# The first stage of a two-block float32 kernel: all 1024 columns of v at once, tile by tile of x

## The chip, the cores and the metric

The kernel runs on one core of a Trainium2 chip. The metric is device microseconds for one execution. Five engines work side by side, each through its own instructions in order: TensorE (PE) for matrix products, VectorE (DVE) and ScalarE (ACT) for elementwise work, GpSimd (POOL), and SyncE (SP), which here issues transfers. They wait for one another through semaphores.

## What is computed

One sequence of 256 tokens with 1024 channels goes through two blocks in float32. The first block has two layers of attention and a feed-forward with a short convolution, the second one a gated delta rule, a retention branch and a feed-forward. The change concerns the start of the first layer:

```python
h = rmsnorm(x, attn_norm[l])
q, k, v = jnp.split(h @ w_qkv_a[l], 3, axis=-1)
q = partial_rope(heads(q, N_HEADS), cos, sin)
k = partial_rope(heads(k, N_HEADS), cos, sin)
o = moba_attention(to_bhsd(q), to_bhsd(k), to_bhsd(heads(v, N_HEADS)))
```

`rmsnorm` multiplies x by a gain per channel and a factor per token, 1/sqrt(mean(x^2) + eps). The angles of the rotation come from `positions`. With 256 tokens the attention is a causal softmax over one block of keys.

## The kernel before

**Products.** x lies transposed on chip, `xT`, as 8 tiles of 128 channels by 256 tokens. Every float32 operand of a large product is split in two parts, hi and lo, and a product is three passes on PE: hi by hi, hi by lo, lo by hi. The weights, 212 MB in all, stream through four buffers `raw` (one transfer fills one, 128x1024 or, at the start, 128x512). ACT makes hi (`emit_hi`, line 188), DVE makes lo by 512 columns (`emit_lo`, line 197), into four buffers each; `ahead` keeps this stream some pieces in front of PE. The parts of x times gain lie in OH and OL.

**Order.** Each engine works through its instructions in the order in which the program's Python issues them. The loop at the end takes a weight piece, issues its products, then lets every running side task (a generator) go one step (`others`), then works ahead on weights. A task's `yield from pause(n)` lets n pieces pass. The tables N_SY and N_STAT say how many pieces the norm's task `stat` lets pass ahead of its sums and ahead of its row products.

**First stage.** x comes in four transfers of two tiles; its gains, `g_attn0`, come with the first parameters in a transfer on ACT's queue. `feed_x` multiplies two tiles by the gain on DVE into TG, splits them, and squares x. The first 512 columns of v take both halves of the tokens over the eight tiles (`X_pair`, two banks of PSUM, `ps_w`), the other 512 follow as two chunks of 256 (`X_chunk`). Meanwhile `stat` sums the squares on PE, makes `tok` on DVE and the factor RTOK on GpSimd, and multiplies RTOK out into rows on PE, which ACT copies to RB. v is evacuated by ACT with the factor RTOK. `angles` makes the angle tables CT and ST in side steps, on DVE with two sines on ACT, then the masks.

**Next stage.** Eight chunks `wqk0` give q and k of two heads each (`W_chunk`). `rope_rows` multiplies the angle tables by RB into CR and SR, `rope` (lines 583 to 586) rotates a chunk on DVE with them, and `attend` does scores, softmax and the product with v, its banks taken from `ps_s` or `ps_d` in turn. The scores of chunks 0 and 1 follow half of chunk 2 on PE.

Of the kernel before, what the change touches and what calls it, by code (L numbers as in the profile page):

```python
# [30 lines left out]
# steps that side work lets pass before it needs what others make for it  # L31
N_RN = (0, 1, 1, 5)
N_SY = (0, 6, 4, 4, 3)
N_STAT = (0, 3, 5, 2, 5)
# [3 lines left out]
N_M1 = (1, 1, 2, 3)  # L38
# [4 lines left out]
PRM = [("g_attn0", 8), ("g_attn1", 8), ("g_kv", 8), ("g_ffn0", 8), ("g_ffn1", 8), ("g_fin", 8),  # L43
# [22 lines left out]
def body(ctx: ExitStack, tc: tile.TileContext, a):  # L66
# [27 lines left out]
    xT = T1([128, 8, T], name="xT")  # L94
# [14 lines left out]
    # the gains first, then x; what is needed later comes behind the first weights  # L109
    nc.scalar.dma_start(prm[:, :PRM_A], a["prm"][:, :PRM_A])  # L110

    def load_x(b):
        nc.sync.dma_start(xT[:, 2 * b:2 * b + 2], a["x"][:, 2 * b:2 * b + 2])
    load_x(0)
    ident = C_("ident")
    ones = T1([128, 1], name="ones")
    V.memset(ones, 1.0)
    warm = T1([128, 1], name="warm")
# [89 lines left out]
    def ahead(i):  # L208
        """what may be loaded and split once the products of piece i are issued"""
# [50 lines left out]
    # tiles that are held over steps: no more of them than the ring has  # L260
# [17 lines left out]
    def wbank(more=0):  # L278
        """two banks in turn; two more while the norm's factors are on their way"""
        if len(deferred) >= 4:  # L280
            drain(cur["stat"])
            late(1)
        wn[0] += 1
        if len(deferred) + more >= 2 and wn[0] % 4 in (3, 0):
            return PT("d")
        return PT("w")

    wn = [0]
# [58 lines left out]
    def N_chunk(src, xs, n, post):  # L347
        """n < 128 columns in a piece"""
# [14 lines left out]
    def D_chunk(grp, src, c, n, ops, post=None, pre=None, done=None):  # L363
        def m(ck, s, hi, lo):
            if c == 0:
                if s == 0:
                    grp.banks = [None] * 4
                    side["dbusy"] = True
                grp.banks[s] = PT("d")
# [20 lines left out]
    def D_tail(grp, src, n, ops, post, pre=None):  # L390
        """the last two chunks, a bank after the other"""
# [18 lines left out]
    def W_pair(src, xs, posts):  # L410
        """two chunks of outputs at once, over the tiles of x"""
# [23 lines left out]
    def X_pair(src, xs, posts):  # L435
        """512 columns, a bank for each half of the tokens"""
# [20 lines left out]

    def slots(t):
        return OH[:, t % 16], OL[:, t % 16]

# [5 lines left out]
    def split(src, hi, lo):  # L466
        """the second part a step after the first"""
# [25 lines left out]
    def sum_ch(out, parts):  # L493
        """sums over the channels, a token per partition; 32 tokens at a time, as the weights' load is what they take"""
# [19 lines left out]
    def renorm():  # L514
        """the splits of x * g * r, for the chunks after the first"""
# [73 lines left out]
    # over the keys of two blocks, for the queries of the second: all of the first, or with the window  # L589
# [4 lines left out]
    # key > query: column > partition  # L594
# [16 lines left out]
    def attend(q, k, v, slot, window=False, sink=None, delay=0, done=False):  # L611
        """q, k: [128, T], a head on each half of the partitions; v(t, half) -> [128, 64]"""
# [38 lines left out]
        for h in range(2):  # L651
# [3 lines left out]
            # blocks: (q0, k0), (q1, k0), (q1, k1)  # L655
# [11 lines left out]
    # ================= the first block =================  # L667
# [7 lines left out]
    def feed_x(b, g, xs, norm, norm2=None, g2=None, first=False):  # L675
        """after xT's pair b is complete: x * g and its splits, the squares"""
        s = slice(2 * b, 2 * b + 2)
        for k in (2 * b, 2 * b + 1):
            cp("V" if first else "V", TG[:, k], xT[:, k], g[:, k:k + 1])
        S.activation(xs[0][:, s], TG[:, s], AF.Copy)  # L680
        if not first:
            sq = square(xT[:, s], norm.room(b))
# [4 lines left out]
        if first:  # L687
            yield
        else:
            yield from pause(3)  # L690
        V.tensor_tensor(xs[1][:, s], TG[:, s], xs[0][:, s].bitcast(F32), op=OP.subtract)
        if first:
            yield
            sq = square(xT[:, s], norm.room(b))
# [13 lines left out]
    # attention of layer 0  # L708
    def v0_pair(t):
        return lambda bank: cp("S", VA[:, t, 0:512], bank, RTOK[:, t:t + 1])  # L710

    def v0_post(c):
        def f(bank):
            for t in range(2):
                S.activation(VA[:, t, c * 256:c * 256 + 256], bank[:, t * T:t * T + T], AF.Copy,
                             scale=RTOK[:, t:t + 1])
        return f
# [15 lines left out]
    X_pair(a["wv0p"], xsR, [v0_pair(t) for t in range(2)])  # L733
    for c in range(2, 4):
        X_chunk(a["wv0"][c - 2], xsR, v0_post(c))
    for j in range(8):
        W_chunk(a["wqk0"][j], xsR, qk0_post(j))
# [30 lines left out]
    def tables():  # L768
        """of the second block"""
# [9 lines left out]
    # feed-forward with a short convolution  # L779
# [63 lines left out]
    # attention of layer 1  # L843
# [45 lines left out]
    # ================= between the blocks =================  # L889
# [7 lines left out]
    def stat2():  # L897
# [4 lines left out]
        # r1 = 1 / sqrt(mean x^2 + eps), and r1 r2 with r2 the factor of x g r1  # L902
# [23 lines left out]
    # ================= the second block =================  # L926
# [10 lines left out]
    def decay_task(bank):  # L937
        # beta and g, a token per partition
# [63 lines left out]
    def conv4(src, u, y, base):  # L1002
        """src, u, y: [128, 2, T]; tiles base[i] of conv_a"""
# [37 lines left out]
    # the small blocks on the diagonal, and the transposes of the inverses  # L1041
# [4 lines left out]
    def delta_task(h, bank):  # L1046
# [180 lines left out]
    # gates of the two branches; they take the decays' place  # L1227
# [10 lines left out]
    # retention  # L1238
# [141 lines left out]
    # residual with a norm behind it: x += y * g * rsqrt(mean(y^2) + eps)  # L1380
# [26 lines left out]
    def to_tok(src, s, banks):  # L1407
        """two tiles of src, a token per partition"""
# [20 lines left out]
    def mix_fin():  # L1429
# [18 lines left out]
        # the first two tiles one by one  # L1448
# [15 lines left out]
    def res_task():  # L1464
# [9 lines left out]
        # the factor r of the feed-forward comes in as r^2: eps / r^4 stands in the norm behind  # L1474
# [17 lines left out]
    # the last feed-forward; its input's factor r comes in at the end, as r^2  # L1492
# [16 lines left out]
    # the products of the last step come with a token per partition, those of its last chunks a half after the other  # L1509
# [61 lines left out]
    # ================= emission =================  # L1571
    # the first pieces of the weights one by one, with the tiles of x between them
    chunks[0].g = 1
    order()
    load_w()
    load_w()
    load_x(1)
    load_w()
    load_w()
    load_x(2)  # L1580
    load_x(3)
    nc.scalar.dma_start(cst[:, :CST_A], a["cst"][:, :CST_A])
    nc.scalar.dma_start(SR.bitcast(I32), a["pos"])
    # the first tiles of x and of the weights by turns
    def more(n):
        for _ in range(n):
            ahead(-1)
    for b in range(4):
        feed(b, P_("g_attn0"), xsR, n0, first=True)
        more(1)  # L1590
        step(fed[b])
        more(N_M1[b])
        if b >= 1:
            drain(fed[b - 1])
    start_stat(n0)
    while ahead(-1):
        pass
    cur["ang"] = start(angles())
# [18 lines left out]
def pack(inp):  # L1617
# [5 lines left out]
    def wc(w, cols):  # L1623
        """[1024, 256 columns] -> [128, 2048]"""
# [5 lines left out]
    def dset(w):  # L1630
        """[K, 1024] -> [K/256, 128, (bank, k tile, 256)]"""
# [4 lines left out]
    def pair(w, cols):  # L1636
        """[1024, 512 columns] -> two of [128, (4 k tiles, 512)]"""
# [6 lines left out]
    def dsett(name, w):  # L1644
        """the last 512 rows as [2, 128, (bank, 4 k tiles, 256)]"""
# [6 lines left out]
    out["x"] = np.ascontiguousarray(A("x")[0].T.reshape(8, 128, T).transpose(1, 0, 2))  # L1652
    out["pos"] = np.ascontiguousarray(np.broadcast_to(A("positions")[0].astype(np.int32)[None], (128, T)))
    w = A("w_qkv_a")[0]
    wsetp("wv0", w, [2048 + 256 * c + r(256) for c in range(4)])
# [44 lines left out]
    def row(v):  # L1700
# [10 lines left out]
        "g_attn0": vec(A("attn_norm")[0]), "g_attn1": vec(A("attn_norm")[1]), "g_kv": vec(A("kv_norm")),  # L1711
# [58 lines left out]
```

## Time and profile before

| | us |
|---|---|
| three runs | 1341.1, 1344.09, 1344.65 |
| median | 1344.09 |
| profiled execution, first to last instruction (its span) | 1341.2 |
| PE busy in it | 1317.4 |
| DVE busy | 984.4 |
| ACT busy | 731.6 |

The page gives the profiled execution by its span alone. In the profile a row of a timeline is a group of equal instructions: its start, how long from its start to the end of its last one, engine, source line, operation, output<-inputs, shapes and count, and in brackets idle time before it with what ended it. Rows of engines overlap, and so do equal instructions that follow each other. PEclk is the clock that PE was granted, as a share of 2.4 GHz.

### The profile page before, as it was taken

The numbers are of one execution on the slowest core, as the hardware profiler recorded it, in microseconds if no ns is written. First come the engines' busy times: TensorE is split into PE (matmuls) and PEld (weight loads), VectorE is DVE, ScalarE is ACT, GpSimd is POOL, SyncE is SP. The second block draws the span as 40 slices with busy tenths as digits, with TensorE's granted clock in tenths as the row PEclk, the third lists the DMA queues.
The fourth block names the chain that finished last, engine by engine and source line by source line (L and its number), as shares of the span: only waits on it lengthen the run. The fifth ranks groups of instructions, "written<-read, shape, count | busy, mean of one in ns | idle before, by whom it ended". The sixth has DMA issues, their size and how long they took to land.

```text
span 1341.2 us, 29103 instructions
## 1 busy us (share of the span) xinstructions
PE 1317.4 (98%) x11824; PEld 1250.3 (93%) x11824; DVE 984.4 (73%) x2225; ACT 731.6 (55%) x1202; POOL 27.2 (2%) x38
## 2 busy tenths in 40 slices
PE   7999999999999999999999999999999999999998
PEld 6999999998889999999888888999999999999996
DVE  6997887778878877788778888666557556855554
ACT  6665765555765655566545544444343445655553
POOL 0000000000000000000000000000000000000000
PEclk9999999998999999999999999999999999999999
DMA  7435565554334655544333333445455564465652
GB/s 240 156 127 183 175 205 188 186 181 142 107 117 156 215 189 189 185 133 158 115 107 114 110 126 104 134 157 191 150 179 168 173 196 153 160 219 184 189 183 89
DMA packets 60470, 215.79 MB, mean 161 GB/s; under 512 B 6832, under 2 KB 7600, under 8 KB 60336
## 3 DMA queue, kind: packets, MB, share of 16 engines
q1 hardware_dynamic: 59328, 212.31, 49.1%
q8 instruction: 93, 1.52, 0.5%
q10 hardware_dynamic: 1008, 1.63, 0.4%
q14 instruction: 41, 0.34, 0.1%
HBM read 212.86 MB, written 1.05 MB: 159 GB/s over the span
## 4 chain that ended last, share of the span: by engine, by line
PE 92%; DVE 4%; ACT 2%; issue 1%; DMA 1%; POOL 0%; SPq 0%; POOLq 0%; DVEq 0%; ACTq 0%
PE ps_w L134 54%; PE ps_d L134 33%; PE ps_s L134 4%; PE ps_s L145 1%; ACT h L634 1%; DVE lo L197 1%; PE ps_d L145 1%; DMA xT<-in_x 0%; DMA raw<-in_wv0p 0%; DVE y L794 0%; ACT hi L188 0%; DVE XL L464 0%; DVE h L626 0%; DVE y L1369 0%; DVE DD L1082 0%
## 5 line engine op out<-in xcount | busy, mean ns | idle before, releaser
L197 DVE TENSOR_TENSOR lo<-raw,hi 128x512 fp32r<-128x512 f32 x801 | 519.7, 684 | 93.5 <-ACT hi L188 92.7
L188 ACT ACTIVATE hi<-raw 128x1024 fp32r<-128x1024 f32 (+1 forms) x403 | 418.1, 1046 | 168.9 <-PE ps_w L134 85.7
L134 PE MATMUL ps_w<-XH,hi 128*128 128x256 f32 x976 | 168.3, 295 | 2.5 <-ACT XH L1454 1.4
L134 PE MATMUL ps_w<-XL,hi 128*128 128x256 f32 x976 | 156.3, 283 | 0.0
L134 PE MATMUL ps_w<-XH,lo 128*128 128x256 f32 x976 | 156.1, 282 | 0.0
L134 PE MATMUL ps_w<-OH,hi 128*128 128x256 f32 x896 | 144.8, 284 | 0.0
L134 PE MATMUL ps_w<-OH,lo 128*128 128x256 f32 x896 | 142.9, 282 | 0.3 <-DVE lo L197 0.3
L134 PE MATMUL ps_w<-OL,hi 128*128 128x256 f32 x896 | 142.5, 281 | 0.0
L134 PEld LDWEIGHTS ps_w<-XH,hi 128*128 128x128 f32 x976 | 134.4, 191 | 7.8 <-ACT XH L1454 1.7
L134 PEld LDWEIGHTS ps_w<-XL,hi 128*128 128x128 f32 x976 | 133.8, 190 | 0.0
L134 PEld LDWEIGHTS ps_w<-XH,lo 128*128 128x128 f32 x976 | 133.6, 190 | 0.0
L134 PE MATMUL ps_d<-OH,hi 128*128 128x256 f32 x776 | 126.0, 283 | 0.0
L134 PEld LDWEIGHTS ps_w<-OH,hi 128*128 128x128 f32 x896 | 121.5, 188 | 3.6 <-issue 3.5
L134 PE MATMUL ps_d<-OL,hi 128*128 128x256 f32 x776 | 124.4, 281 | 0.0
L134 PE MATMUL ps_d<-OH,lo 128*128 128x256 f32 x776 | 124.3, 281 | 0.0
L134 PEld LDWEIGHTS ps_w<-OH,lo 128*128 128x128 f32 x896 | 122.1, 189 | 0.5 <-DVE lo L197 0.5
L134 PEld LDWEIGHTS ps_w<-OL,hi 128*128 128x128 f32 x896 | 121.7, 188 | 0.0
L134 PEld LDWEIGHTS ps_d<-OH,hi 128*128 128x128 f32 x776 | 104.9, 188 | 1.9 <-issue 1.7
L134 PEld LDWEIGHTS ps_d<-OL,hi 128*128 128x128 f32 x776 | 105.1, 187 | 0.3 <-DVE OL L470 0.2
L134 PEld LDWEIGHTS ps_d<-OH,lo 128*128 128x128 f32 x776 | 105.1, 188 | 0.2
L790 ACT ACTIVATE y<-u,prm 128x256 f32<-128x256 f32 x88 | 48.0, 595 | 62.4 <-DVE u L764 62.4
L764 DVE TENSOR_TENSOR u<-ps_w,RB 128x512 f32<-128x512 f32 x44 | 30.1, 689 | 63.0 <-PE ps_w L134 56.8
(378 smaller groups left out, 1644.7 us busy)
## 6 DMA issues: line engine op xcount, KB each, us to landing
raw<-in_wu SPq DMA_DIRECT2D x108, 512.0 KB, 4.2
raw<-in_wd SPq DMA_DIRECT2D x68, 512.0 KB, 3.9
raw<-in_wgb SPq DMA_DIRECT2D x24, 512.0 KB, 3.7
raw<-in_wqk SPq DMA_DIRECT2D x16, 512.0 KB, 4.0
raw<-in_wza SPq DMA_DIRECT2D x16, 512.0 KB, 3.8
raw<-in_wqkb SPq DMA_DIRECT2D x16, 512.0 KB, 4.1
raw<-in_wbra SPq DMA_DIRECT2D x16, 512.0 KB, 4.2
raw<-in_wbrb SPq DMA_DIRECT2D x16, 512.0 KB, 4.7
```

The costliest lines, as they stand in the source:

```text
L134: PE.matmul(out, lhsT, rhs, start=start, stop=stop, skip_group_check=True)
L145: PE.transpose(out, in_, ident)
L188: S.activation(hi[:, :w], raws[n][:, :w], AF.Copy)
L197: V.tensor_tensor(lo[:, c], raws[n][:, c], hi[:, c].bitcast(F32), op=OP.subtract)
L634: S.activation(e[h][:, c], e[h][:, c], AF.Exp, bias=nm[:, i:i + 1], accum_out=sums[:, i:i + 1])
L764: V.tensor_tensor(u, v2(bank), bc(RB, 2), op=OP.mult)
L790: S.activation(y[:, i], u[:, i], AF.Identity, bias=P_(cb, t), scale=P_(cw, 3 * t + 2))
```

## The change

- v's 1024 columns are worked on together, x tile by x tile (`X_quad`): four banks, two of `ps_w` and two of `ps_d`, for two halves of the tokens and two halves of the columns. They are all evacuated at the end of the stage. The first chunk of q and k takes a bank of `ps_d`.
- The gains of the first norm stand in front of x in one array. The first transfer brings them with tile 0; then come tile 1, tiles 2 and 3, and tiles 4 to 7, with weights between. The remaining parameters, constants and positions follow on SP's queue, where they were on ACT's.
- OH and OL are made from x (`split_gain`): ACT multiplies by the gain while it converts, DVE makes the low part in one instruction. Tiles 0 to 3 are split ahead of the loop, tiles 4 to 7 and all squares are steps of a side task, `feed_first`.
- Two float32 products of a vector of ones, 128 by 512, which nothing reads, stand first on PE.
- N_SY and N_STAT of the first norm are 1 and 2, before 6 and 3. Banks while a norm's factors are awaited are chosen by another rule (`wbank`); outside the first layer this changes no instruction's place.

The core of the diff (comments that were taken out are not shown):

```diff
-N_SY = (0, 6, 4, 4, 3)
-N_STAT = (0, 3, 5, 2, 5)
+N_SY = (0, 1, 4, 4, 3)
+N_STAT = (0, 2, 5, 2, 5)
-N_M1 = (1, 1, 2, 3)
+WARM = 2
+X_FIRST = 4
...
-    xT = T1([128, 8, T], name="xT")
+    xg = T1([128, 8 + 8 * T], name="xT")
+    xT = xg[:, 8:].rearrange("p (k t) -> p k t", k=8)
...
-    nc.scalar.dma_start(prm[:, :PRM_A], a["prm"][:, :PRM_A])
-    def load_x(b):
-        nc.sync.dma_start(xT[:, 2 * b:2 * b + 2], a["x"][:, 2 * b:2 * b + 2])
-    load_x(0)
+    def load_x(k, n):
+        c = slice(8 + k * T if k else 0, 8 + (k + n) * T)
+        nc.sync.dma_start(xg[:, c], a["x"][:, c])
+    load_x(0, 1)
...
+    idle = PT("s")
+    for _ in range(WARM):
+        PE.matmul(idle, ones.to_broadcast([128, 128]), ones.to_broadcast([128, 512]), start=True, stop=True, skip_group_check=True)
...
-        if len(deferred) >= 4:
+        if len(deferred) + more >= 6:
             drain(cur["stat"])
-            late(1)
-        wn[0] += 1
-        if len(deferred) + more >= 2 and wn[0] % 4 in (3, 0):
-            return PT("d")
-        return PT("w")
+            late()
+        return PT("w" if len(deferred) + more < 2 else "d")
...
+    def X_quad(src, xs, posts):
+        xh, xl = xs
+        banks = {}
+        def mk(k0):
+            def m(ck, s, hi, lo):
+                k, g = k0 + s // 2, s % 2
+                todo = []
+                for t in range(2):
+                    if k == 0:
+                        banks[t, g] = PT("d" if g else "w")
+                    tt = slice(t * 128, t * 128 + 128)
+                    todo.append((banks[t, g], xh[:, k, tt], xl[:, k, tt], hi, lo, k == 0, k == 7))
+                products(todo, True)
+            return m
+        def done(ck):
+            drain(cur["stat"])
+            for g in range(2):
+                for t in range(2):
+                    wpost(posts[t, g])(banks[t, g])
+        first = add(Chunk(src[:, :1024], 1024, 2, mk(0)))
+        first.g = 1
+        add(Chunk(src[:, 1024:], 7168, 14, mk(1), None, {13: done}))
...
+    def feed_first():
+        def sq(b):
+            n0.feed(b, square(xT[:, 2 * b:2 * b + 2], n0.room(b)))
+        for k in range(X_FIRST, 8):
+            split_gain(k, xg[:, k:k + 1], xsR[0][:, k], xsR[1][:, k])
+            yield
+            if k % 2:
+                sq(k // 2 - 2)
+            yield
+        for b in range(2, 4):
+            sq(b)
+            yield
+        start_stat(n0)
...
-    X_pair(a["wv0p"], xsR, [v0_pair(t) for t in range(2)])
-    for c in range(2, 4):
-        X_chunk(a["wv0"][c - 2], xsR, v0_post(c))
+    X_quad(a["wv0"], xsR, {(t, g): v0_post(t, g) for t in range(2) for g in range(2)})
     for j in range(8):
-        W_chunk(a["wqk0"][j], xsR, qk0_post(j))
+        W_chunk(a["wqk0"][j], xsR, qk0_post(j), None, "d" if j == 0 else None)
...
+    for k, n in ((1, 1), (2, 2), (4, 4)):
+        load_w()
+        if k == 1:
+            load_w()
+        load_x(k, n)
+    nc.sync.dma_start(prm[:, :PRM_A], a["prm"][:, :PRM_A])
+    nc.sync.dma_start(cst[:, :CST_A], a["cst"][:, :CST_A])
+    nc.sync.dma_start(SR.bitcast(I32), a["pos"])
+    for k in range(X_FIRST):
+        split_gain(k, xg[:, k:k + 1], xsR[0][:, k], xsR[1][:, k])
+        for _ in range(4 if k == 0 else 2):
+            ahead(-1)
     while ahead(-1):
         pass
+    cur["stat"] = start(feed_first())
```

How the order moves is seen at three places. First SP's queue at the start of the program (in_x is x, in_wv0p and in_wv the weights of v, prm parameters, cst constants, SR the positions). Before:

```order
L113 DMA xT<-in_x 128x512
L182 DMA raw<-in_wv0p 128x512 x2
L113 DMA xT<-in_x 128x512
L182 DMA raw<-in_wv0p 128x512 x2
L113 DMA xT<-in_x 128x512 x2
L182 DMA raw<-in_wv0p 128x1024 x2
```

and now:

```order
L114 DMA xT<-in_x 128x264
L187 DMA raw<-in_wv 128x512 x2
L114 DMA xT<-in_x 128x256
L187 DMA raw<-in_wv 128x1024
L114 DMA xT<-in_x 128x512
L187 DMA raw<-in_wv 128x1024
L114 DMA xT<-in_x 128x1024
L1607 DMA prm<-in_prm 128x64
L1608 DMA cst<-in_cst 128x384
L1609 DMA SR<-in_pos 128x256
L187 DMA raw<-in_wv 128x1024 x4
```

The constants and positions now stand in front of the fifth weight transfer, which is the first 128x1024 row behind them.

Second, DVE around `tok`, from which RTOK is made (lines 559 to 569 before, 588 to 598 now, are the angles; lo<-raw,hi is the stream of weights). Before, from the first 128x1024 weights on:

```order
L197 TENSOR_TENSOR lo<-raw,hi 128x512 x4
L559 CAST CT<-SR 128x256
L560 TENSOR_SCALAR ST<-CT,prm 128x256
L197 TENSOR_TENSOR lo<-raw,hi 128x512 x3
L537 TENSOR_SCALAR tok_274<-ps_s 128x2
L197 TENSOR_TENSOR lo<-raw,hi 128x512 x2
L562 TENSOR_SCALAR CR<-ST 128x256
L563 TENSOR_SCALAR CR<-CR 128x256
```

and now, from the last fold of the squares on:

```order
L516 TENSOR_TENSOR nacc<-nacc 128x256
L591 TENSOR_SCALAR CR<-ST 128x256
L592 TENSOR_SCALAR CR<-CR 128x256
L202 TENSOR_TENSOR lo<-raw,hi 128x512 x4
L595 SCALAR_TENSOR_TENSOR ST<-CR,ST 128x256 x3
L596 TENSOR_SCALAR ST<-ST 128x256
L597 SCALAR_TENSOR_TENSOR CT<-ST 128x256
L598 TENSOR_SCALAR CT<-CT 128x256
L566 TENSOR_SCALAR tok_339<-ps_s 128x2
L202 TENSOR_TENSOR lo<-raw,hi 128x512 x6
```

`tok` stood behind two instructions of the angles and now stands behind all of them.

Third, ACT from the copy of RB on (line 188 before and 193 now convert weights; REG<-ps evacuates v; CT and ST are the two sines). Before:

```order
L542 COPY RB<-ps_s 128x256
L138 ACTIVATE REG<-ps_w,RTOK 128x512 x2
L188 ACTIVATE hi<-raw 128x1024
L715 ACTIVATE REG<-ps_d,RTOK 128x256 x2
L188 ACTIVATE hi<-raw 128x1024 x2
L571 ACT_TABLE_LOAD
L571 ACTIVATE CT<-CT 128x256
L572 ACTIVATE ST<-ST 128x256
L715 ACTIVATE REG<-ps_w,RTOK 128x256 x2
L188 ACTIVATE hi<-raw 128x1024 x5
```

and now:

```order
L571 COPY RB<-ps_s 128x256
L193 ACTIVATE hi<-raw 128x1024
L600 ACT_TABLE_LOAD
L600 ACTIVATE CT<-CT 128x256
L601 ACTIVATE ST<-ST 128x256
L143 ACTIVATE REG<-ps_w,RTOK 128x512 x2
L143 ACTIVATE REG<-ps_d,RTOK 128x512 x2
L193 ACTIVATE hi<-raw 128x1024 x5
```

The evacuations stood apart, conversions between them, the first two ahead of the sines; now all four stand in a row behind the sines.

## Rows read from the trace of the kernel before

**Rows 1.** The page: busy shares of the engines, and the conversion of weights on ACT.

```profile
PE 1317.4 (98%) x11824; PEld 1250.3 (93%) x11824; DVE 984.4 (73%) x2225; ACT 731.6 (55%) x1202; POOL 27.2 (2%) x38
...
L188 ACT ACTIVATE hi<-raw 128x1024 fp32r<-128x1024 f32 (+1 forms) x403 | 418.1, 1046 | 168.9 <-PE ps_w L134 85.7
```

**Rows 2.** Timeline of the start: start us, us to the end, engine, line, instruction.

```profile
4.33 0.62 DVE L142 TENSOR_SCALAR REG<-xT,prm 128x256 f32<-128x256 f32 x2 [3.38 <-DMA prm<-in_prm]
...
5.53 0.63 ACT L188 ACTIVATE hi<-raw 128x512 fp32r<-128x512 f32 x1
...
6.21 1.22 PE L134 MATMUL ps_w<-hi,OH 128*128 128x512 f32 x2 [6.21 <-ACT hi L188]
...
9.79 1.05 PE L134 MATMUL ps_w<-hi,OL 128*128 128x512 f32 x2
...
10.65 1.05 PE L134 MATMUL ps_w<-lo,OH 128*128 128x512 f32 x2
...
15.98 2.50 DVE L197 TENSOR_TENSOR lo<-raw,hi 128x512 fp32r<-128x512 f32 x4 [0.24 <-ACT hi L188]
...
16.00 0.73 PE L134 MATMUL ps_w<-hi,OH 128*128 128x512 f32 x2 [1.11 <-ACT hi L188]
...
17.50 0.63 PE L134 MATMUL ps_w<-hi,OH 128*128 128x512 f32 x2
...
17.96 0.63 PE L134 MATMUL ps_w<-hi,OL 128*128 128x512 f32 x2
```

**Rows 3.** What the DMA engines moved, GB/s in 40 slices of 1 us from 0.

```profile
GB/s 0 33 177 300 313 358 405 352 373 430 373 332 307 209 256 338 205 72 201 315 205 315 229 254 369 238 274 307 225 234 4 0 0 139 324 291 287 217 250 82
```

**Rows 4.** Timeline from the norm's sums to the first use of q and k.

```profile
20.39 0.22 PE L134 MATMUL ps_s<-ones,nacc 128*32 128x1 f32 x2
...
21.30 0.72 PE L134 MATMUL ps_w<-hi,OH 128*128 128x512 f32 x2
...
21.65 1.08 POOL L538 TENSOR_TENSOR RTOK<-tok,mhalf 128x2 f32<-128x2 f32 x1 [21.21 <-DVE tok L537]
...
26.01 0.37 ACT L542 COPY RB<-ps_s 128x256 f32<-128x256 f32 x1 [1.53 <-PE ps_s L145]
...
26.28 1.27 ACT L138 ACTIVATE REG<-ps_w,RTOK 128x512 f32<-128x512 f32 x2
...
29.14 1.34 DVE L566 SCALAR_TENSOR_TENSOR ST<-CR,ST 128x256 f32<-128x256 f32 x3
...
31.30 0.29 DVE L569 TENSOR_SCALAR CT<-CT 128x256 f32<-128x256 f32 x1
...
32.28 1.28 ACT L571 ACT_TABLE_LOAD   x1
...
34.22 0.63 PE L134 MATMUL ps_w<-OH,hi 128*128 128x256 f32 x4
34.42 0.84 ACT L715 ACTIVATE REG<-ps_w,RTOK 128x256 f32<-128x256 f32 x2
...
36.85 0.35 DVE L574 TENSOR_SCALAR ST<-ST,prm 128x256 f32<-128x256 f32 x1
...
40.34 0.74 DVE L583 STREAM_SHUFFLE u<-ps_w 128x512 f32<-128x512 f32 x1
...
45.78 0.01 DVE L583 LOAD_MASK_SELECT u<-ps_w  x1 [0.40 <-PE ps_w L134]
...
48.50 1.03 PE L134 MATMUL ps_d<-qk 64*128 64x128 f32 x9
```

**Rows 5.** Windows of 1 us: busy us of each engine (instructions), PEclk, DMA share, GB/s.

```profile
323.00:324.00 1.00, 0.00 (x0) 0.00 (x0) 1.00 (x3) 0.00 (x0) 0.99 (x1) 1.00 0.79 180
324.00:325.00 1.00, 0.00 (x0) 0.00 (x0) 0.67 (x2) 0.00 (x0) 1.00 (x1) 1.00 0.86 332
...
326.00:327.00 1.00, 1.00 (x9) 1.00 (x8) 0.76 (x2) 1.00 (x3) 0.00 (x0) 0.73 0.83 156
...
333.00:334.00 1.00, 1.00 (x10) 1.00 (x9) 1.00 (x2) 0.68 (x1) 0.00 (x0) 0.86 0.00 0
```

More of the change, by code (lines that the diff above doesn't have):

```diff
@@ L41 @@
 QB_HEADS = [(p, 4 + p) for p in range(4)] + [(8 + p, 12 + p) for p in range(4)]
-PRM = [("g_attn0", 8), ("g_attn1", 8), ("g_kv", 8), ("g_ffn0", 8), ("g_ffn1", 8), ("g_fin", 8),
+PRM = [("g_attn1", 8), ("g_kv", 8), ("g_ffn0", 8), ("g_ffn1", 8), ("g_fin", 8),
        ("g_mixpre", 8), ("g_mixpost", 8), ("g_mlppre", 8),
@@ L278, in wbank @@
     def wbank(more=0):
-        if len(deferred) >= 4:
+        if len(deferred) + more >= 6:
             drain(cur["stat"])
-            late(1)
-        wn[0] += 1
-        if len(deferred) + more >= 2 and wn[0] % 4 in (3, 0):
-            return PT("d")
-        return PT("w")
-    wn = [0]
+            late()
+        return PT("w" if len(deferred) + more < 2 else "d")
     def waiting():
@@ L366, in m @@
                 if s == 0:
+                    if deferred:
+                        drain(cur["stat"])
+                        late()
                     grp.banks = [None] * 4
@@ L456, in X_pair @@
         add(Chunk(src[1], 2048, 4, mk(1), None, {3: done}))
+    def X_quad(src, xs, posts):
[13 more added lines that the diff above has]
+        def done(ck):
+            drain(cur["stat"])
+            for g in range(2):
[4 more added lines that the diff above has]
+        add(Chunk(src[:, 1024:], 7168, 14, mk(1), None, {13: done}))
     def slots(t):
@@ L673, in body, with feed_x @@
     fed = {}
-    def feed_x(b, g, xs, norm, norm2=None, g2=None, first=False):
+    def feed_x(b, g, xs, norm, norm2=None, g2=None):
         s = slice(2 * b, 2 * b + 2)
         for k in (2 * b, 2 * b + 1):
-            cp("V" if first else "V", TG[:, k], xT[:, k], g[:, k:k + 1])
+            cp("V", TG[:, k], xT[:, k], g[:, k:k + 1])
         S.activation(xs[0][:, s], TG[:, s], AF.Copy)
-        if not first:
-            sq = square(xT[:, s], norm.room(b))
+        sq = square(xT[:, s], norm.room(b))
         if norm2:
@@ L686, in feed_x @@
                 S.activation(sq2[:, i * T:i * T + T], xT[:, 2 * b + i], AF.Square, scale=g2[:, 2 * b + i:2 * b + i + 1])
[L687 to L690, printed above, removed]
+        yield from pause(3)
         V.tensor_tensor(xs[1][:, s], TG[:, s], xs[0][:, s].bitcast(F32), op=OP.subtract)
-        if first:
-            yield
-            sq = square(xT[:, s], norm.room(b))
         norm.feed(b, sq)
@@ L706, in body, with v0_post @@
     n0 = Norm()
[L709 to L717, printed above, removed]
+    def feed_first():
[11 more added lines that the diff above has]
+        start_stat(n0)
+    def v0_post(t, g):
+        return lambda bank: cp("S", VA[:, t, 512 * g:512 * g + 512], bank, RTOK[:, t:t + 1])
     att = {}
@@ L1569, in body @@
         m_down(c)
-    chunks[0].g = 1
     order()
[L1575 to L1586, printed above, removed]
-            ahead(-1)
[L1588 to L1595, printed above, removed]
+    for k, n in ((1, 1), (2, 2), (4, 4)):
[9 more added lines that the diff above has]
+        for _ in range(4 if k == 0 else 2):
+            ahead(-1)
     while ahead(-1):
         pass
+    cur["stat"] = start(feed_first())
     cur["ang"] = start(angles())
@@ L1651, in pack @@
     out = {}
-    out["x"] = np.ascontiguousarray(A("x")[0].T.reshape(8, 128, T).transpose(1, 0, 2))
+    x = A("x")[0].T.reshape(8, 128, T).transpose(1, 0, 2).reshape(128, -1)
+    out["x"] = np.ascontiguousarray(np.concatenate([A("attn_norm")[0].reshape(8, 128).T, x], axis=1))
     out["pos"] = np.ascontiguousarray(np.broadcast_to(A("positions")[0].astype(np.int32)[None], (128, T)))
     w = A("w_qkv_a")[0]
-    wsetp("wv0", w, [2048 + 256 * c + r(256) for c in range(4)])
+    out["wv0"] = np.ascontiguousarray(w[:, 2048:].reshape(8, 128, 1024).transpose(1, 0, 2).reshape(128, -1))
     out["wqk0"] = wset(w, [np.concatenate([128 * j + r(128), 1024 + 128 * j + r(128)]) for j in range(8)])
@@ L1710, in pack @@
     vals = {
-        "g_attn0": vec(A("attn_norm")[0]), "g_attn1": vec(A("attn_norm")[1]), "g_kv": vec(A("kv_norm")),
+        "g_attn1": vec(A("attn_norm")[1]), "g_kv": vec(A("kv_norm")),
         "g_ffn0": vec(A("ffn_norm")[0]), "g_ffn1": vec(A("ffn_norm")[1]), "g_fin": vec(A("final_norm")),
```

## Prediction

> **What bounds the kernel now.** I read the page's busy shares first: TensorE (PE) is busy 98% of the span [rows 1]. So the change pays only if it ends a PE wait or a slow stretch of PE, and if what PE gains is not waited away behind it. Then the timeline of the start. PE's first product begins at 6.21 us, released by the first converted weight piece (0.63 on ACT, from 5.53). Two products of 128x512 start every 0.86 us there (9.79, 10.65), which is the 1.2 GHz level, though the profile's clock column reads 1.00 in that stretch; from 17.50 to 17.96 two take 0.46, the 2.4 GHz level. PE waits 1.11 us before 16.00 for one more conversion [rows 2]. The stage over v ends when the first product of the q/k stage starts, at 34.22 [rows 4].
>
> Third, the timeline up to the first use of q and k, because a lead of PE at 34.2 counts only if it arrives there. At 48.50 PE multiplies the rotated q and k of chunks 0 and 1; the rotation of chunk 1 started on DVE at 45.78, after DVE had waited 0.40 us for PE [rows 4]. So before, PE and DVE come to this place nearly together, PE the later by 0.4. Whatever makes PE earlier here makes DVE the one that is waited for.
>
> **The change, part by part.** It starts PE sooner (one DMA of 135 KB carries x's first tile and the gains; no multiply on DVE stands ahead of the first conversion) and sends two unread products ahead. The stage's useful products cover the same columns: 96 of 512 in place of 48 of 512 and 96 of 256. At 0.233 us each that is 22.4 us, with 0.9 for the norm's sums (20.39 to 21.30) [rows 4].
>
> *Start.* Up to the end of the first weight piece 0.40 MB have to be moved, before 0.56 MB with two more DMAs beside them. By the row of GB/s, 0.40 MB have moved at 3.6 us [rows 3]; the landing comes about 1 us behind that (before, the first 0.30 MB had moved at 3.3, and DVE was released at 4.33 [rows 2]). With the conversion, the first product comes at 5.3, 0.9 earlier. Bounds: 4.8 and 6.2.
>
> *Unread products.* Two f32 products of 512 columns, from about 0.9 us on. No row shows one. Below: as the product of this kernel at the low level, 0.43 each; above: eight times that, 6.9 us in all, to 7.8. I take four passes each, 3.4 us, ended by 4.4 and hidden by the wait for DMA. If they lift the clock, the real products start at 2.4 GHz; if not, PE stays low for as long as before, from 5.3 to about 11.5, which costs 3.1 us.
>
> *PE up to the norm's factors.* The order now puts 14 of 16 pieces (84 products, 19.6 us) and the sums (0.9) ahead of the two row products that need RTOK. From 5.3 that is 25.8 at the high level, 28.9 with the low one until 11.5.
>
> *The factors.* Here the stage stops. RTOK is made from DVE's tok, and tok now stands behind the angle block on DVE. DVE's work up to tok hangs on the fifth weight load. Ahead of it in the one queue are 1.05 MB of x, 1.57 MB of weights and 0.36 MB of constants; with itself 3.51 MB, moved at 12.2 [rows 3], landed at 13.2. Its conversion takes 1.05 [rows 1] and one part of x on ACT 0.4; DVE goes on at 14.6. From there to tok it has: 11 low parts of weights at 0.60 (2.50 for four, the last in full) [rows 2], 6.6; three low parts of x, priced as the scalar_tensor_tensor of 256 columns at 0.45 (1.34 for three), 1.3; two adds at 0.60 and a fold of 0.4, 1.6; four steps on 256 columns at 0.30, 1.2; the angle block from 29.14 to 31.59, 2.45 [rows 4]. Sum 13.2: tok at 27.8, then 0.1 and 1.08 on GpSimd, RTOK at 29.0. PE waits there 3.2 us at the high level, 0.1 at the low one. So the clock of the first products is worth next to nothing, and the unread products with it. The row products end at 29.3, the last piece (1.4) at 30.7: the stage is over 3.5 us sooner than at 34.22.
>
> *What is late next.* ACT stands in order behind the same factors: the copy of RB at 29.4 (0.37), a conversion 1.0, the table load with two sines 2.14 (32.28 to 34.42), now all four evacuations of v in a row (1.27 for two, so 2.5), then the conversion of the weights of chunk 1's second half, 1.05: it ends at 36.5. On DVE one low part (0.6) waits for that, and behind it stand the sign, the masks, a low part and the two products with RB, 3.49 (36.85 to 40.34) [rows 4]. The rotation of chunk 0 starts at 40.6, before at 40.34. That rotation and four low parts take 5.04 (5.44 less the wait of 0.40): chunk 1 at 45.6 against 45.78, and q and k are used 2.7 later, at 48.3 against 48.50. PE's own way there is 14.3 long (34.22 to 48.50); from 30.7 it is there at 45.0 and waits 3.3 us. What was gained in the first stage is handed back here. Behind it PE is the busy engine and waits for nothing long, so the end moves by what this place moves: -0.2 us.
>
> *The rest.* In layer 0's attention the same instructions follow in the same order, but for the bank (ps_s or ps_d) that takes a head's products; from there on nothing is moved. I price the banks at 0, since PE's waits of before come from elsewhere; bounds -0.5 and +1. Bounds of the whole: the fifth load may land at 12.2 (no lag) or 14.5 (small rows of constants slow the queue, or the second part of the parameters, for which one of DVE's four steps waits, is late by as much); the dense runs of DVE and ACT, some 24 us, may be 5% quicker or slower than priced, 1.2. Together -2.7 to +3.3.
>
> **A rule against the change.** The profile shows one other long gap of PE: it does nothing at 323 to 325 and the clock is granted at 0.50, the 1.2 GHz level, from within 326 until within 333 [rows 5]. The Trainium skill, TensorE: Matmul & The Clock Gate, "HAM oscillation — how this bites in real kernels", says that waits between bursts of products throttle PE again, so that the next burst starts cold; the trace agrees, with that 0.50. By the rule the gap of 3.3 us before 48.3 is not only a gap; it makes rival 2.
>
> **Rivals.** (1) PE keeps its lead: 3.5 us, 1340.6. For it: DVE has idle time ahead of the rotation (3.38 us before 4.33 alone [rows 2]), which could cover the queue. Against: the order; tok stands behind 13 us of work that cannot begin before the fifth load is there, and ACT's 7 us behind RB are strict. It decides if that load lands by 11 and ACT's run is 2 shorter. Without the wait for RTOK, at the high level, the stage would end at 27.5 and the time be 1337.4; I give that almost nothing. (2) Slower: the gap before 48.3 (or that before RTOK) brings the clock down, as at 323. There the low stretch lasted 6.8 us (326.5 to 333.3 by the means of 0.73 and 0.86) [rows 5]; half of that is lost, 3.4 us, so +3.2, 1347.3. Part of it is free if PE waits for the softmax behind anyway. It decides if a gap of more than the 2 us of rows 5 stays, and it passes 0.3% only if the low stretch is over 8 us or falls twice. (3) The transfers bound the start: the constants ahead of the fifth load hold it to 14.5, and all behind moves with it: +1.1, 1345.2.
>
> **How the numbers follow.** The profiled execution spans 1341.2; the page gives no other time of it, and the runs read 1341.1, 1344.09 and 1344.65, so what lies around the span is 0 to 3.5 us. I set the -0.2 against the median: 1344.1 - 0.2 = 1343.9. Chances: the lead is handed back (forecast) 0.62, rival 1 0.14, rival 2 0.16, rival 3 0.08. A difference of 0.3%, 4.0 us, is about what a measurement here tells from no change. Rival 1 passes it in some half of its cases, rival 2 in half of its, and the forecast with the spread of medians in one of ten, to either side: faster 0.13, same 0.75, slower 0.12. The range for 8 in 10 takes the forecast's bounds with 0.7 of spread below and reaches to rival 2 above: 1340.5 to 1347.5; it just takes in rival 1.
>
> **What would show it.** In the profile after: the first useful product near 5.3 us; PE idle before the two row products until RTOK at about 29, if the clock was high; the q/k stage begun near 30.7; four evacuations of v in a row on ACT, and a conversion behind them ending near 36.5; the rotation of chunk 1 at 45 to 47, with no wait of DVE for PE, and PE idle for 2 to 4 us before the products of q and k at about 48.3; from there the times of before. The forecast is wrong if PE starts these products before 46.5, if RTOK is there before 27, if the first stage ends after 33, or if a clock of 0.50 stands between 46 and 56.

## The result, and the profile after

The changed kernel takes 1350.62 us (median of 4 runs, 1350.18 to 1352.21) against 1343.87 of the kernel before: a ratio of 1.0055, 95% interval 1.0041 to 1.0069. It is slower by half a per cent, where I had forecast no change (1343.9, range 1340.5 to 1347.5).

The page of the profile after, first the span and PE's share, which answer to [rows 1]:

```profile
span 1348.9 us, 29012 instructions
...
PE 1327.8 (98%) x11780; PEld 1258.4 (93%) x11780; DVE 982.3 (73%) x2221; ACT 731.6 (54%) x1203; POOL 27.5 (2%) x38
```

PE makes fewer products than before (11780 for 11824) and is busy 10.4 us longer. So the time is not in a wait. The timeline after, at the places of [rows 2] and [rows 4] (PE, POOL, ACT and DVE put together in order of time; start us, us to the end):

```profile
0.91 3.52 PE L122 MATMUL ps_s<-ones 128*128 128x512 f32 x4 [0.91 <-DVE ones L118]
4.82 0.74 PE L139 MATMUL ps_w<-hi,OH 128*128 128x512 f32 x2 [0.38 <-ACT hi L193]
...
10.13 0.73 PE L139 MATMUL ps_w<-hi,OH 128*128 128x512 f32 x2 [2.25 <-ACT OH L492]
...
28.88 0.15 DVE L566 TENSOR_SCALAR tok<-ps_s 128x2 f32<-128x2 f32 x1
...
29.11 1.08 POOL L567 TENSOR_TENSOR RTOK<-tok,mhalf 128x2 f32<-128x2 f32 x1 [28.68 <-DVE tok L566]
...
31.38 0.37 ACT L571 COPY RB<-ps_s 128x256 f32<-128x256 f32 x1 [3.56 <-PE ps_s L150]
...
32.56 0.64 PE L139 MATMUL ps_d<-OH,hi 128*128 128x256 f32 x4
...
32.73 1.28 ACT L600 ACT_TABLE_LOAD   x1
...
36.93 2.96 ACT L193 ACTIVATE hi<-raw 128x1024 fp32r<-128x1024 f32 x3
...
42.13 0.73 DVE L612 STREAM_SHUFFLE u<-ps_d 128x512 f32<-128x512 f32 x1
...
47.09 0.73 DVE L612 STREAM_SHUFFLE u<-ps_w 128x512 f32<-128x512 f32 x1
...
47.52 0.93 PE L139 MATMUL ps_d<-qk 64*128 64x128 f32 x8
...
49.77 0.37 PE L139 MATMUL ps_d<-qk 64*128 64x128 f32 x1 [1.32 <-DVE qk L615]
```

The first stage ends at 32.56 in place of 34.22, and the rotation of chunk 1 starts 1.3 us later than before (47.09 against 45.78), where I had forecast it 0.2 us sooner. PE waits 1.32 us for its q and k, where I had forecast 3.3. So the lead of the first stage is handed back, and 1.3 us with it, of the 7.7 by which the spans differ; the rotation of chunk 2 is still 1.3 us late (57.06 against 55.77). The rest comes later, in stages whose instructions the change does not move. GpSimd's steps mark the same places of both programs; ahead the kernel before, behind it the changed one:

```profile
131.56 0.99 POOL L538 TENSOR_TENSOR RTOK<-tok,mhalf 128x2 f32<-128x2 f32 x1 [107.49 <-DVE tok L537]
...
323.01 2.21 POOL L538 TENSOR_TENSOR RTOK<-tok,mhalf 128x2 f32<-128x2 f32 x1 [190.46 <-DVE tok L537]
...
1149.81 0.70 POOL L1437 TENSOR_TENSOR RM<-tok,mhalf 128x2 f32<-128x2 f32 x1 [74.69 <-DVE tok L1436]
```

```profile
133.31 0.99 POOL L567 TENSOR_TENSOR RTOK<-tok,mhalf 128x2 f32<-128x2 f32 x1 [101.91 <-DVE tok L566]
...
327.19 2.21 POOL L567 TENSOR_TENSOR RTOK<-tok,mhalf 128x2 f32<-128x2 f32 x1 [192.90 <-DVE tok L566]
...
1158.88 0.69 POOL L1465 TENSOR_TENSOR RM<-tok,mhalf 128x2 f32<-128x2 f32 x1 [75.10 <-DVE tok L1464]
```

From the first to the second of these places 191.45 us went by before and 193.88 after, 2.43 more; to the third 826.80 and 831.69, 4.89 more, although the slow clock of before at 326 to 333 [rows 5] is missing after; behind it 191.4 and 190.0, 1.4 less. In the first of these stretches, from 134 to 320 us, PE waits for nothing in either kernel and its clock is 1.00. What differs is its pace, the interval from the start of one product to the start of the next. Groups of four products of 256 columns, before and after (the first operand in a row is the stationary one, which is loaded into PE; the second, the moving one, streams through it):

```profile
200.08 0.64 PE L134 MATMUL ps_w<-OL,hi 128*128 128x256 f32 x4
...
203.39 0.64 PE L134 MATMUL ps_w<-OH,lo 128*128 128x256 f32 x4
```

```profile
199.88 0.64 PE L139 MATMUL ps_d<-OL,hi 128*128 128x256 f32 x4
...
203.24 0.64 PE L139 MATMUL ps_w<-OH,lo 128*128 128x256 f32 x4
```

Seven groups lie between the two rows each time: 3.31 us before, 118.2 ns a product; 3.36 after, 120.0. Product by product the pattern differs too: after, nearly every interval from 150 to 320 us is 120 ns; before, they go round between 115 and 123, with a mean of 118.3. In the last stage, where the pieces of weights are the stationary operand and OH, OL the moving one (512 columns), it is the other way round, and there the changed kernel gains:

```profile
1250.05 0.63 PE L134 MATMUL ps_d<-hi,OH 128*128 128x512 f32 x2
...
1252.85 0.63 PE L134 MATMUL ps_d<-hi,OH 128*128 128x512 f32 x2
```

```profile
1250.28 0.62 PE L139 MATMUL ps_d<-hi,OH 128*128 128x512 f32 x2
...
1251.64 0.62 PE L139 MATMUL ps_d<-hi,OH 128*128 128x512 f32 x2
```

Before it is 2.80 us for six pairs, 233 ns a product; after, 1.36 for three, 227.

The same instructions on the same data at another pace: I looked for what the change does to them without touching them. It takes g_attn0 out of PRM and puts its 8 columns in front of x in the tile xT. Tiles lie one behind the other in the order in which they are made. So xT is 32 bytes longer, prm 32 shorter, and the tiles between (XH, XL, OH, OL, REG) and the start of prm stand 32 bytes further on, all others where they were: OH at 41,088 before and 41,120 after, hi at 128,672 in both programs.

### The profile page after: what moved, and what is told of

It reads as the page before. It is cut to its first block, busy times and chain, and to the rows that moved or that the text cites. A ratio compares the mean times of both kernels' runs of the same rounds, so it can differ in the third digit from the quotient of the medians.

```text
span 1348.9 us, 29012 instructions
## 1 busy us (share of the span) xinstructions
PE 1327.8 (98%) x11780; PEld 1258.4 (93%) x11780; DVE 982.3 (73%) x2221; ACT 731.6 (54%) x1203; POOL 27.5 (2%) x38
## 4 chain that ended last, share of the span: by engine, by line
PE 91%; DVE 5%; ACT 2%; issue 1%; DMA 0%; POOL 0%; SPq 0%; POOLq 0%; DVEq 0%; ACTq 0%
PE ps_w L139 52%; PE ps_d L139 33%; PE ps_s L139 4%; DVE lo L202 1%; PE ps_s L150 1%; ACT h L663 1%; PE ps_d L150 1%; DVE h L655 0%; DMA raw<-in_wv 0%; ACT hi L193 0%; DVE y L822 0%; DVE XL L493 0%; DVE y L1397 0%; DVE DD L1110 0%; DVE y L1396 0%
## 5 line engine op out<-in xcount | busy, mean ns | idle before, releaser
L193 ACT ACTIVATE hi<-raw 128x1024 fp32r<-128x1024 f32 (+2 forms) x402 | 418.0, 1048 | 172.6 <-PE ps_w L139 74.9
L139 PE MATMUL ps_d<-OH,hi 128*128 128x256 f32 (+1 forms) x792 | 129.9, 285 | 0.0
L139 PE MATMUL ps_d<-OL,hi 128*128 128x256 f32 (+1 forms) x792 | 128.4, 283 | 0.0
L139 PE MATMUL ps_d<-OH,lo 128*128 128x256 f32 (+1 forms) x792 | 128.3, 283 | 0.0
L139 PEld LDWEIGHTS ps_d<-OH,hi 128*128 128x128 f32 (+1 forms) x792 | 108.8, 191 | 2.0 <-issue 1.7
L139 PEld LDWEIGHTS ps_d<-OL,hi 128*128 128x128 f32 (+1 forms) x792 | 108.9, 191 | 0.3
L139 PEld LDWEIGHTS ps_d<-OH,lo 128*128 128x128 f32 (+1 forms) x792 | 108.9, 191 | 0.2
```

Of the source, the lines that this page charges most:

```text
L139: PE.matmul(out, lhsT, rhs, start=start, stop=stop, skip_group_check=True)
L193: S.activation(hi[:, :w], raws[n][:, :w], AF.Copy)
```

## The experiments

Below, "distance" is the address of hi less that of OH, mod 256. It is the same for XH, XL, OL and lo, which lie multiples of 256 bytes from these: 32 before, 0 after. The pace is the mean interval of 256-column products from 150 to 320 us.

**Addresses alone.** Unused tiles push the others on. In before_s32:

```diff
     xT = T1([128, 8, T], name="xT")
+    T1([128, 8], name="pad1")
...
     REG = T1([128, 4096], name="REG")
+    T1([128, 8], name="pad2")
```

after_s0 has the same two lines in the changed kernel (pad1 behind xg); before_s32_w0 has pad1 alone; before_w0 has pad2 alone, behind lvl.

> The changed kernel with XH, XL, OH, OL and REG back on a multiple of 64 bytes (an unused tile of 32 bytes ahead of them and one behind; the pieces of weights stay at 32 mod 64, as in both kernels). Theory A (the 32 bytes of gains in front of x push the five tiles to 32 mod 64, and PE's pace hangs on that): in the stretch from 150 to 320 us products of 256 columns start every 118.3 ns in the mean, as before, not every 120.0, and the time is 1343 to 1346. Rival B (the unread products or the clock of the first 15 us put PE in another mode that then lasts): 120.0 ns and 1350.6. Rival C (the new place of the instructions in the stream): 120.0 ns and 1350.6.

> The kernel before with nothing but addresses moved: XH, XL, OH, OL, REG at 32 mod 64, as in the changed kernel, all other tiles at the place mod 64 that they had. Theory A: products of 256 columns every 120.0 ns from 150 to 320 us, those of 512 columns every 226.7 in place of 233.3, time 1350 to 1352. Rivals B and C: 118.35 ns, 1343.9.

> The kernel before, XH to REG at 0 mod 64 as they were, but all that lies behind the constants (the pieces of weights raw, hi, lo among it) moved by 32 bytes, to 0 mod 64. Theory A1 (the place of the stationary tiles alone decides): 118.35 ns, 1343.9. Theory A2 (it decides whether weights and activations stand at the same place within 64 bytes, as in the changed kernel): 120.0 ns, 1350 to 1352. Rivals B and C: 118.35, 1343.9.

> The kernel before, XH to REG at 32 mod 64 and the pieces of weights at 0 mod 64: the fourth of the four combinations. Theory A1: 120.0 ns, 1350 to 1352. Theory A2: 118.35 ns, 1343.9. Rivals B and C: 118.35, 1343.9.

after_s0: 118.3 ns and 1342.18 us, 0.9994 of the kernel before (0.9985 to 1.0003). The loss is gone, with every instruction of the change in place; rivals B and C fall. Its GpSimd steps:

```profile
132.05 0.99 POOL L569 TENSOR_TENSOR RTOK<-tok,mhalf 128x2 f32<-128x2 f32 x1 [100.81 <-DVE tok L568]
...
323.50 2.21 POOL L569 TENSOR_TENSOR RTOK<-tok,mhalf 128x2 f32<-128x2 f32 x1 [190.46 <-DVE tok L568]
```

191.45 us again, to the hundredth what it was before.

Two of the other three missed what theories A, A1 and A2 expected of them: before_s32 gave 113.4 ns and 1311.09 us (0.976, 0.9746 to 0.9775), before_w0 113.4 and 1315.01 (0.9792, 0.9775 to 0.9809). before_s32_w0 gave 118.3 and 1343.22 (1.000, 0.9991 to 1.0009), as A2 had it and A1 had not; but before_w0 speaks against both. So neither the place of the stationary tiles nor the place within 64 bytes decides. The runs fall in line by the distance: 32 in the kernel before, after_s0 and before_s32_w0; 64 in before_s32 (the pads move OH by 32 and hi by 64) and in before_w0; 0 in the changed kernel. Nine groups in before_w0:

```profile
199.84 0.62 PE L135 MATMUL ps_w<-OL,hi 128*128 128x256 f32 x4
...
203.47 0.62 PE L135 MATMUL ps_w<-OH,hi 128*128 128x256 f32 x4
```

3.63 us for eight of them, 113.4 ns. An empty tile of 32 bytes makes the kernel before 2.1% faster. That is a lucky find: both runs were made to bring the loss about or to leave the time alone.

**The distance, and the pair of operands.** The kernel before with pad2 behind REG of 16, 24, 40 and 56 columns (distances 96, 128, 192, 256); in before_lo64 a pad between hi and lo:

```diff
         if c == 0:
+            if n == 0:
+                TW([128, 8], "pad2", 1)
             parts[n].append(TW([128, 1024], "lo", LA + 1, F32R))
```

> The kernel before with the pieces of weights 64 bytes further on: distance from OH to hi 96 mod 512 (before 32; the changed kernel 0; before_s32 and before_w0 64). Theory A3 (the distance mod 128 decides, the same to both sides, so 96 is as 32): products of 256 columns every 118.3 ns from 150 to 320 us, 1343. Rival A4 (the further apart the better): under 113.3 ns, 1311 or less.

> The kernel before with the pieces of weights 96 bytes further on: distance from OH to hi 128 mod 512. Theory A3 (distance mod 128): as the changed kernel, 120.0 ns and 1350. Rival A4 (the further apart the better): 113.3 ns or less, 1311 or less.

> The kernel before with the pieces of weights 160 bytes further on: distance 192 from OH to hi. Measured so far from 150 to 320 us: 120.0 ns at distance 0, 118.3 at 32, 113.4 at 64, 117.3 at 96, 118.7 at 128. If the pace goes roughly with the distance mod 128: 113.4 ns and 1311. If 64 is a single low place: 117 to 120 ns and 1338 to 1351.

> The kernel before with the pieces of weights 224 bytes further on: distance 256. If the pace goes with the distance mod 256: 120.0 ns and 1350, as the changed kernel; if it goes with it mod 128: 118.7 ns and 1344, as before_d128; if neither: something else.

> The kernel before with 32 bytes between the tiles hi and lo: hi stays at distance 32, lo goes to 64 (all tiles behind lo move by 32 bytes too). If the pace of a product is set by the addresses of its own two operands: products with lo start 113.4 ns after one another, those with hi every 118.3 as before, and a third of the gain of before_w0 is there, 1332 to 1336. If it is a matter of the layout as a whole: one pace for all products, 118.3 or 113.4.

Then the places between, with 32 and 48 columns for pad2 (160, 224), and hi and lo begun 16 bytes inside their tiles (48; with before_w0's pad 80):

```diff
-        hi = TW([128, 1024], "hi", LA + 1, F32R)
+        hi = TW([128, 1088], "hi", LA + 1, F32R)[:, 4:]
```

> The kernel before with hi and lo read and written 16 bytes further on (their tiles 256 bytes wider, the first 16 bytes unused): distance 48. If the pace falls evenly from 118.3 ns at 32 to 113.4 at 64: 115 to 117 ns and 1325 to 1332. If it goes by steps of 32 bytes: 118.3 and 1343, or 113.4 and 1313.

> before_w0 with hi and lo 16 bytes further on: distance 80. If 64 is the low place of a curve that rises evenly to 117 to 118 at 96: 115 to 116 ns, 1322 to 1332. If there is a lower place between 64 and 96: under 113.4 ns, under 1311. By steps of 32 bytes: 113.4 and 1313.

> The kernel before with the pieces of weights 128 bytes further on: distance 160. Between 118.7 ns at 128 and 117.8 at 192, if the curve is even there: 117.8 to 118.7 and 1333 to 1345. If distances of 64 and 160 pair (two low places in 256 bytes): 113 to 115 ns and 1311 to 1322.

> The kernel before with the pieces of weights 192 bytes further on: distance 224, that is 32 short of 256, which gave 120.0 ns. If the pace is the same to both sides of 0 mod 256: 118.3 ns and 1343, as at 32. If the order of the two addresses counts: something between 117.8 (at 192) and 120.0 (at 256), but not the pattern of before.

What was measured, with the PE instructions that the windows view counts from 200 to 300 us. Each ratio is to the kernel before as timed beside that run, where its median was 1343.1 to 1344.0 us:

| distance | kernel | ns | PE x, 200 to 300 | us | ratio (95%) |
|---|---|---|---|---|---|
| 0 | after | 120.0 | 836 | 1350.62 | 1.0055 (1.0041 to 1.0069) |
| 32 | before | 118.3 | 848 | 1343.87 | 1 |
| 48 | before_d48 | 118.3 | 847 | 1344.00 | 1.0012 (0.9993 to 1.0031) |
| 64 | before_w0 | 113.4 | 885 | 1315.01 | 0.9792 (0.9775 to 0.9809) |
| 80 | before_d80 | 118.7 | 845 | 1345.44 | 1.0013 (1.0000 to 1.0027) |
| 96 | before_d96 | 117.3 | 855 | 1340.70 | 0.9980 (0.9972 to 0.9989) |
| 128 | before_d128 | 118.7 | 846 | 1343.73 | 1.0005 (0.9997 to 1.0014) |
| 160 | before_d160 | 120.0 | 836 | 1355.45 | 1.0098 (1.0075 to 1.0121) |
| 192 | before_d192 | 117.8 | 852 | 1333.54 | 0.9925 (0.9905 to 0.9945) |
| 224 | before_d224 | 116.7 | 859 | 1331.40 | 0.9914 (0.9888 to 0.9939) |
| 256 | before_d256 | 120.0 | 835 | 1353.37 | 1.0072 (1.0052 to 1.0093) |

A3 and A4 both fall: 64 and 192 differ, 0 and 128 differ, and 64 is a single narrow place, with 48 and 80 as slow as before. At 80, 160 and 224 the pace is none of those that had been expected, and no rule that was put forward gives the whole row of figures. The one pair 256 apart (0 and 256) agrees, to 120 ns for nearly every product. In before_d48 and before_d80 the pieces lie 4352 bytes apart in place of 4096, so that every second one is 256 bytes further off, and the pace is one, 118.3 and 118.7 ns; at other distances it was not tried. The time does not follow the pace of this stretch alone. At 192 it falls by 0.75% where the pace falls by 0.5%: there the products with XH and XL as stationary operand, which stand in later stages, start every 116.8 ns in the mean, in the kernel before every 118.3. Why one distance gives two paces stays open.

In before_lo64 hi stays at distance 32 and lo goes to 64:

```profile
200.65 0.63 PE L134 MATMUL ps_w<-OL,hi 128*128 128x256 f32 x4
201.11 0.62 PE L134 MATMUL ps_w<-OH,lo 128*128 128x256 f32 x4
201.57 0.64 PE L134 MATMUL ps_w<-OH,hi 128*128 128x256 f32 x4
202.05 0.63 PE L134 MATMUL ps_w<-OL,hi 128*128 128x256 f32 x4
```

The four with lo take 0.46 us, the eight with hi 0.94: over 150 to 320 us the intervals from lo's products to the next have a mean of 114.0 ns, those from hi's of 118.1. So the pace goes by the piece that a product reads, and not by the layout as a whole. It is not wholly a matter of the single product: OH by hi now has 119.9 ns and OL by hi 116.3, where the kernel before has 118.5 and 118.3, though their places are the same. The time, 1331.82 (0.9916, 0.9899 to 0.9932), holds a third of before_w0's gain and a little more.

**The changed kernel at distance 64, and its hand-back.** after_d64 has a pad2 of 16 columns behind REG; after_d64_sines also the angles' steps at other pauses; after_s0_nowarm is after_s0 with WARM = 0:

```diff
-        yield from pause(4)
+        yield from pause(3)
         V.tensor_scalar(kq, ang, float(np.float32(0.15915494309189535)), MAGIC, op0=OP.mult, op1=OP.add)
...
-        yield from pause(4)
+        yield from pause(3)
         for c in (c1, c2, c3):
...
-        yield from pause(3)
+        yield from pause(2)
         S.activation(CT, pf, AF.Sin)
```

> The changed kernel with one unused tile of 64 bytes behind REG: distance 64 from OH to hi, all else as it was. If the distance is the whole of the matter: 113.3 ns in place of 120.0 and 1309 to 1312, as before_s32 with the change's own effect of about nothing (after_s0 against the kernel before: 0.9994). If the changed kernel is slower for another reason besides: over 1315.

> after_d64 with the angles' pauses 4, 3, 3, 2, 3 in place of 4, 4, 4, 3, 3: the sines stand on ACT ahead of the copy of RB, the sign and the masks on DVE behind three low parts after tok. Theory L (the first stage's lead is handed back on ACT and DVE between RB and the rotation): the rotation of chunk 0 starts at 37 to 39 us in place of 41 to 42, q and k are used 2 to 3.5 us sooner than in after_d64, and the time is 1.5 to 3.5 us less than that of after_d64. Rival (the rotation waits for PE or the weights anyway): rotation of chunk 1 within 0.5 us of after_d64, time the same.

> after_s0 without the two unread products. Theory L (what PE gains in the first stage is handed back before q and k are used): the first stage ends 0 to 3.5 us later, the products of q and k start within 1 us of after_s0, and the time is that of after_s0 within 0.15%. Rival (the early start of PE's clock is worth its low products): 1.5 to 3.5 us slower than after_s0.

after_d64: 113.4 ns, 1312.46 us (0.9773, 0.9760 to 0.9785), 0.5 above what was expected and within the noise of before_s32 (0.976, 0.9746 to 0.9775). At this distance, too, the two kernels cannot be told apart by their time.

after_d64_sines: 1311.33 us (0.9766, 0.9750 to 0.9783). Its rotations, and the use of q and k, chunk 1 behind chunk 0 without a wait (eight products in after's row at 47.52, nine here):

```profile
38.23 0.75 DVE L613 STREAM_SHUFFLE u<-ps_d 128x512 f32<-128x512 f32 x1
...
43.66 0.01 DVE L613 LOAD_MASK_SELECT u<-ps_w  x1 [0.39 <-PE ps_w L140]
...
46.27 1.03 PE L140 MATMUL ps_d<-qk 64*128 64x128 f32 x9
```

In after_d64 the rotations start at 42.43 and 47.40, and chunk 1 is used at 50.08. So the ACT and DVE work between RB and the rotation is what hands the lead back: once it lies earlier, DVE waits for PE again (0.39), and the next rotation is 3.7 us sooner (53.65 against 57.38). Of that 2.9 is left at the end of the two profiled spans (1310.3 and 1307.4). The medians differ by 1.1, less than the runs scatter (1309.31 to 1315.22), and less than the 1.5 to 3.5 expected: the time does not resolve it.

after_s0_nowarm: 1343.35 us, 1.0009 of after_s0's median. The first stage ends at 31.96 in place of 31.77, chunk 1 of q and k is 0.2 later. The unread products are worth 0.2 us there and nothing that the time shows, as theory L expects.

## Why the prediction was wrong

**The step that failed** is "The rest": "from there on nothing is moved. I price the banks at 0 ... bounds -0.5 and +1." I followed instructions and banks, and not addresses. The term is +8.2 us (1.0055 of the kernel before against after_s0's 0.9994; the medians, 1350.62 and 1342.18, differ by 8.4), eight times the upper bound of that step, and no rival was near it. The layout could be read from the full diff: a tile 8 columns wider ahead of five others, a tile 8 columns narrower behind them.

The Trainium skill, SBUF — State Buffer, "Who interferes with whom", gives PE two read ports, one for the moving operand and one for weight loads, and calls them independent. By that I would expect the distance to change nothing; the measurement decides otherwise, 120.0 ns at 0 and 113.4 at 64. Whether it is at these ports that the two operands meet, no run here shows.

None of the signs that I had named for a wrong forecast appeared: the products of q and k start at 47.52, RTOK is there at 30.2, the first stage ends at 32.56, and the clock is 1.00 from 46 to 56. All four lie in the first 56 us, and most of the loss lies behind. The bounds of the whole do not reach 8 either (of the two, +3.3 counts the forecast's -0.2 in, and -2.7 leaves it out).

**The steps of the start** held, each within 2 us, all but the first product later than forecast or at the forecast time. Start times in us: forecast, after, after_s0:

| step | forecast | after | after_s0 |
|---|---|---|---|
| unread products ended | 4.4 | 4.43 | 4.69 |
| first product | 5.3 | 4.82 | 4.78 |
| fifth weight load landed | 13.2 | 14.3 | 14.1 |
| tok | 27.8 | 28.88 | 28.72 |
| first stage over | 30.7 | 32.56 | 31.77 |
| rotation of chunk 0 | 40.6 | 42.13 | 41.31 |
| rotation of chunk 1 | 45.6 | 47.09 | 46.28 |
| chunk 1 of q, k used | 48.3 | 49.77 | 48.95 |

The queue of work behind the fifth weight load is as long as priced (DVE dense from 15.88 to tok, 13.0 us for 13.2), but starts 1.3 later: DVE waits 1.55 us there for a part of x that ACT comes to at 15.36 only, behind the conversion of that load at 14.39. The 2.25 us of PE before 10.13 are of that kind too: on ACT a conversion of weights that waited for its DMA until 8.62 stands ahead of x's second tile. RB comes 2.0 later than priced (31.38 for 29.4), and the lead is handed back as forecast. The gap of PE there is smaller than the 3.3 of the forecast, 1.32 and 0.23: PE comes to the products of q and k at 47.52 in place of 45.0, and those of chunk 0 take 0.9 of the time until chunk 1 is rotated. I had read the nine products at 48.50 [rows 4] as the use of both chunks; eight are chunk 0's, and chunk 1's first starts at 49.26 in the kernel before. Against that, chunk 1 is used 0.5 us later in the changed kernel and 0.3 sooner in after_s0.

Without the address, the lead is handed back for the reasons I gave, and the time of after_s0, 0.9994 of the kernel before, is near the -0.2 us of the forecast; that it is so near is in part luck. In its profiled execution the rotation of chunk 1 comes 0.5 us later than before (46.28 against 45.78), and the GpSimd steps stay 0.49 behind up to 323 us. Then the slow clock of 326 to 333 is shorter (1.00 again from 330 on), and the step at 1149.81 comes at 1149.12. before_s32_w0, whose start is that of the kernel before, goes the same way, from 0.62 behind (132.18) to 0.77 ahead (1149.04). So differences of this size belong to the single execution, and the sign of the change's own effect is not shown.

**Rival 2** (a gap lowers the clock) was right in kind, at another place. After the 2.25 us without products PE's clock falls to 0.50, the 1.2 GHz level; windows of 1 us, PEclk the third number from the end:

```profile
9.00:10.00 1.00, 0.00 (x0) 0.00 (x0) 0.29 (x1) 1.00 (x2) 0.00 (x0) 1.00 1.05 430
...
11.00:12.00 1.00, 1.00 (x3) 0.81 (x4) 0.54 (x2) 1.00 (x2) 0.00 (x0) 0.50 1.07 404
...
13.00:14.00 1.00, 1.00 (x3) 0.72 (x3) 1.00 (x3) 0.03 (x1) 0.00 (x0) 0.50 1.02 414
```

In after_s0 a gap of 1.84 at the same place (7.84 to 9.68) left the clock at 1.00, and so did, in the changed kernel, the gap of 1.32 before chunk 1's products, of which the rival spoke; in after_d64 and after_d64_sines gaps of 2.58 and 2.11 at the first place brought it down. The norm's sums come at 27.19 in the changed kernel and at 25.88 in after_s0; at the use of chunk 1 of q and k 0.8 us of that are left. **Rival 1** (the lead is kept) fails in the kernel as changed and is what after_d64_sines makes of it. **Rival 3** (the transfers hold the fifth load to 14.5) has its condition nearly met: the load landed at 14.3 (issued at 7.63, 6.7 us to landing), in after_s0 at 14.1, and ACT waits for it there:

```profile
14.18 1.06 ACT L195 ACTIVATE hi<-raw 128x1024 fp32r<-128x1024 f32 x1 [1.45 <-DMA raw<-in_wv]
```

That accounts for the 1.1 by which tok is late; it lies within the bounds that I gave the load (12.2 to 14.5). The rival's +1.1 us is not in the time: in after_s0 the rotation of chunk 1 is 0.7 later than forecast, too little for the time to resolve. Whether the constants or the other transfers ahead held the load was not tried.

## What to carry to other kernels

When a change makes a tile wider, narrower or new, compare the addresses of all tiles before and after, the stationary and moving operands of the main products above all; a time that moves evenly over stages whose code is unchanged points there. Name signs of a wrong forecast for the stages, too, that the change leaves alone. To tell a change from its layout, time it again with unused tiles that put the old distances back. And where PE is the bound, try some distances for themselves: 32 to 64 bytes of padding gave 2.1 to 2.4% here, where the change itself gave nothing that can be measured.

## What was not expected of the hardware

- The pace of fp32r products depends on the distance of the two operands' addresses: 256-column products every 113.4 ns at distance 64, 116.7 to 118.7 at most others, 120.0 at 0, 160 and 256, at a granted clock of 1.00 throughout (150 to 320 us). For 512 columns with the operands' roles exchanged the mean from 1180 to 1300 us is 227.9 ns at distance 0, 228.9 at 64 and 233.3 at 32: the slowest distance of the one is the quickest of these for the other, and 64 is good for both.
- The effect is local to the operands (114.0 and 118.1 ns side by side in before_lo64) and does not depend on where the pair lies (two different placements at distance 64, three at 32, each with one pace in this stretch). Whether the stationary operand that counts is a product's own or that of the next one cannot be told: OH and OL lie alike.
- By which mechanism the distance acts, and why 64 is so narrow, stays open: the traces show the pace, not the reads.
